# A 31-tap convolution on VectorE as three 16-tap filters over half the outputs each, in a hybrid encoder layer

## The chip, the core and the metric

One core of one Trainium2 chip runs the whole layer. The metric is the device time of one execution in microseconds (us). Two timed runs of the kernel before gave 1527.39 and 1528.0 us, median 1527.7. One more execution was profiled: it took 1526.56 us, and its instructions span 1524.8 us. All rows below come from that execution, with times counted from its first instruction.

## What is computed

The layer takes x (2048 tokens by 1024 channels, float32) and a conditioning vector c:

- h = RMSNorm(x) * (1 + scale(c)) + shift(c), then z = h @ W_in, cut into six parts of 1024 columns: a, a_glu, a_gate, u, v, b_gate.
- Group A: a * sigmoid(a_glu); then a depthwise convolution of 31 taps along the tokens (every channel has its own 31 weights, 15 tokens of zero padding on either side) plus a bias; then LayerNorm over the channels, silu, times silu(a_gate).
- Group B: u * (W_s LN(v) + b) over chunks of 128 tokens, times silu(b_gate).
- out = RMSNorm(x + gate(c) * (concat(A, B) @ W_out)).

For the change only the convolution matters, and the way the kernel forms its matrix products in the stage before it. With g the padded input of one channel and w its weights, the convolution is y[t] = bias + sum over i of w[i] * g[t + i], i = 0 to 30.

## The kernel before, in words

**Stages.** The tokens are handled in two halves of 1024 (hf = 0, 1). For each half the kernel forms h, then v (v_half), then runs 20 units: eight conv_in units (a and a_glu for channel block j of 128), eight gmlp units (u and b_gate) and four conv_gate units (a_gate). After both halves comes the output stage: the 16 token tiles of 128 are put into five groups of 3, 4, 4, 3 and 2 (GROUPS). The products of Group B's columns with W_out for groups 1 to 4 go first, and their partial sums are stored (part_out). Then for each group in turn Group A's rows are normalised (norm, a generator whose pieces are started by step() between tiles), split and multiplied (by_rows for group 0, by_tile for the others), and out_tile adds the residual, normalises and stores.

**A unit.** One unit makes two blocks of 128 output channels for 1024 tokens with seven products M1 to M7 (a Strassen-like scheme, L370 to L399), each of them 12 matmuls of 512 columns, because each operand is kept as a high and a low part (split, L129). It uses three PSUM banks p, t, q out of six. On TensorE the order is M1, then M4 of the unit before it (flush), M5, M6, M2, M3, M7. Before the change ScalarE copies M1 from p to SBUF (m1, L379), TensorE makes M6 in q, VectorE adds m1 to q in place (L384), ScalarE copies the sum out (u2, L385), and M7 later accumulates onto q.

**The convolution.** conv(hf, j) (L417) handles one channel block of one half. It loads g from DRAM (dG, written by conv_in), starts acc on ScalarE with the first tap and the bias (L429), adds the other 30 taps on VectorE, each one scalar_tensor_tensor over all n outputs (L431), and stores acc to DRAM (dC, L432). The first half's outputs end at token CUT = 1008, so that they need only the first half's input; the second half has 1040. There are two g buffers (pool gc) and one acc buffer (pool acc). The loads and the store of conv are issued by the POOL queue, one behind the other: the store of block j stands before the load of block j + 2.

**Order of work.** A scheduler orders each engine's instructions when the kernel is built, by priority and by its own simulated times; each engine then runs its list in that order. conv is under low() (tc.high_priority with an offset of -6000): its instructions come after any other work that is ready at that time, and so fill what VectorE has free. norm(2), the normalisation for tokens 896 to 1407, needs the convolution of all eight channel blocks of both halves, as do norm(3) and norm(4); norm(0) and norm(1) need the first half alone.

**Other users of the buffers touched.** Pool ct (five tiles of 128x512 before) holds m1, m5, u2 of the units, vm of gmlp, the raw weights of v_half (rv), Group B's rows on the way to the output stage (yb), and tm of out_tile.

Of the kernel before, what the change touches and what calls it, by code (L numbers as in the profile page):

```python
# [8 lines left out]
F32 = mybir.dt.float32  # L9
F32R = mybir.dt.float32r  # L10
AF = mybir.ActivationFunctionType
ALU = mybir.AluOpType
# [3 lines left out]
P = 128  # L16
D = 1024
KC = D // P
KH = KC // 2
S = 2048  # L20
T = 1024
NTT = T // P
W = 31
# [1 line left out]
EPS = 1e-6  # L25
NG = 512
LATE = 6000
CUT = T - PAD - 1
CSPAN = [(0, CUT), (CUT, S - CUT)]
GROUPS = [(0, 3), (3, 4), (7, 4), (11, 3), (14, 2)]  # L30

# [7 lines left out]
def hybrid_layer_kernel(  # L39
# [29 lines left out]
    gcp = pool("gc", 2)  # L69
    accp = pool("acc", 1)  # L70
    vcp = pool("vc", 1)
    ctp = pool("ct", 5)
    sqp = pool("sq", 1)
    tabs = pool("tabs", 2)
    small = pool("small", 4)
# [13 lines left out]
    def ct(name, dt=F32):  # L89
        return ctp.tile([P, NG], dt, tag="ct", name=name)  # L90
# [16 lines left out]
    c_sb = const.tile([P, KC], F32, name="c_sb")  # L107
    bss_sb = const.tile([P, KC, 2], F32, name="bss_sb")
    cw_sb = const.tile([P, KC, W], F32, name="cw_sb")
    ident = const.tile([P, P], F32, name="ident")  # L110
    ones = const.tile([P, P], F32, name="ones")
    csil = const.tile([P, KC], F32, name="csil")
# [170 lines left out]
    def v_half(hf, between=lambda: None):  # L283
        for r, pairs in enumerate(((("A11", "B1"), ("A12", "B2")), (("S1", "B1"), ("A22", "Bd")))):
            name = f"v{hf}{r}"
            ps = [[(bank if 2 * t + g < 6 else xbank)(f"pv_{hf}_{r}_{t}_{g}") for g in range(2)] for t in range(4)]
            for k in range(KH):
                for i, (b, typ) in enumerate(pairs):
                    for g in range(2):
                        s = v_op(typ, k, g, name)  # L290
                        st, sp = (k, i) == (0, 0), (k, i) == (KH - 1, 1)
                        for t in range(4):
                            a0, a1 = (H[b, k][:, q, t * P : (t + 1) * P] for q in range(2))
                            nc.tensor.matmul(ps[t][g], a0, s[:, 0, :], start=st, stop=False)
                            nc.tensor.matmul(ps[t][g], a0, s[:, 1, :], start=False, stop=False)
                            nc.tensor.matmul(ps[t][g], a1, s[:, 0, :], start=False, stop=sp)
            if r == 0:
                between()
            st = sm(f"vst_{name}", 16)
            sums, mean, var = st[:, 0:8], st[:, 8:12], st[:, 12:16]  # L300
            sq = sm(f"vsq_{name}", 8)
            vt = []
            for t in range(4):
                v = flat(slot(f"vt_{name}_{t}"))
                for g in range(2):
                    act(v[:, g * NG : (g + 1) * NG], ps[t][g], AF.Copy, accum_out=sums[:, 4 * g + t : 4 * g + t + 1])
                vt.append(v)
            TT(out=mean, in0=sums[:, 0:4], in1=sums[:, 4:8], op=ALU.add)
            TS(out=mean, in0=mean, scalar1=-1.0 / D, scalar2=None, op0=ALU.mult)
            for t in range(4):  # L310
                for g in range(2):
                    act(
                        ct(f"vq_{name}_{t}_{g}"),
                        vt[t][:, g * NG : (g + 1) * NG],
                        AF.Square,
                        bias=mean[:, t : t + 1],
                        accum_out=sq[:, 4 * g + t : 4 * g + t + 1],
                    )
            TT(out=var, in0=sq[:, 0:4], in1=sq[:, 4:8], op=ALU.add)
            TS(out=var, in0=var, scalar1=1.0 / D, scalar2=EPS, op0=ALU.mult, op1=ALU.add)  # L320
            rs = rstd_of(var, 4, name)
            nmr = sm(f"nmr_{name}", 4)
            TT(out=nmr, in0=mean, in1=rs, op=ALU.mult)
            for t in range(4):
                act(vt[t], vt[t], AF.Identity, bias=nmr[:, t : t + 1], scale=rs[:, t : t + 1])
                nc.sync.dma_start(dV[hf][4 * r + t].rearrange("p j d -> p (j d)"), vt[t])
# [30 lines left out]
    def product(ps, m, s, first):  # L357
        for k in range(KH):
            h = H[BLK[m], k]
            w0, w1 = (s[:, q, k * P : (k + 1) * P] for q in range(2))  # L360
            mm = lambda w, a, st, sp: nc.tensor.matmul(ps, w, a, start=st, stop=sp, skip_group_check=True)  # L361
            mm(w0, h[:, 0, :], first and k == 0, False)
            mm(w0, h[:, 1, :], False, False)
            mm(w1, h[:, 0, :], False, k == KH - 1)
# [7 lines left out]
    def unit(hf, key, cx, cy, start, finish):  # L372

        name = f"{hf}_{key[0]}{key[1]}"
        ws = weights(key, cx, cy, name)
        p, t, q = (bank(f"p{n}_{name}") for n in "ptq")
        m1, m5, u2 = (ct(f"{n}_{name}") for n in ("m1", "m5", "u2"))
        product(p, "M1", next(ws), True)
        act(m1, p, AF.Copy)  # L379
        flush()  # L380
        product(t, "M5", next(ws), True)
        act(m5, t, AF.Copy)
        product(q, "M6", next(ws), True)
        TT(out=q, in0=q, in1=m1, op=ALU.add)  # L384
        act(u2, q, AF.Copy)  # L385
        product(p, "M2", next(ws), False)
        y = start()
        product(t, "M3", next(ws), False)
        TT(out=y[:, :NG], in0=t, in1=u2, op=ALU.add)
        product(q, "M7", next(ws), False)  # L390
        TT(out=y[:, NG:], in0=q, in1=m5, op=ALU.add)
        last = next(ws)

        def rest():
            product(q, "M4", last, False)
            finish(p, q, y)

        pending.append(rest)
# [18 lines left out]
    def conv(hf, j):  # L417
        c0, n = CSPAN[hf]
        with low():
            g = gcp.tile([P, 1072], F32, tag="gc", name=f"gc_{hf}_{j}")  # L420
            if hf == 0:
                nc.gpsimd.memset(g[:, 0:PAD], 0.0)
                nc.gpsimd.dma_start(g[:, PAD : PAD + T - 1], dG[0][j][:, : T - 1])
            else:
                nc.gpsimd.memset(g[:, n + PAD : n + 2 * PAD], 0.0)
                nc.gpsimd.dma_start(g[:, : 2 * PAD + 1], dG[0][j][:, c0 - PAD :])
                nc.gpsimd.dma_start(g[:, 2 * PAD + 1 : n + PAD], dG[1][j])
            acc = accp.tile([P, 1040], F32, tag="acc", name=f"acc_{hf}_{j}")[:, :n]
            act(acc, g[:, 0:n], AF.Identity, bias=convb[:, j : j + 1], scale=cw_sb[:, j, 0:1])  # L429
            for i in range(1, W):  # L430
                STT(out=acc, in0=g[:, i : i + n], scalar=cw_sb[:, j, i : i + 1], in1=acc, op0=ALU.mult, op1=ALU.add)  # L431
            nc.gpsimd.dma_start(dC[hf][j], acc)  # L432

    def conv_gate(hf, i):
# [185 lines left out]
        for k in range(KH):  # L620
            H[b, k] = None
    c_row = vcp.tile([P, D], F32, tag="vc", name="c_row")
    rows0 = accp.tile([P, 1040], F32, tag="acc", name="rows0")[:, :D]
    nc.sync.dma_start(c_row[0:1, :], c[None, :])
    nc.gpsimd.memset(ones, 1.0)
    act(sm("warm", 1), ones[:, 0:1], AF.Silu)
# [13 lines left out]
    def x_home(hf):  # L640

        xs = []
        for k in range(KH):
            if k < 2:
                t = rawp.tile([P, 2, D], F32, tag="raw", name=f"x{hf}_{k}")
                xs.append((t[:, 0, :], t[:, 1, :]))
            elif k == 2:
                xs.append([hpool.tile([P, D], F32, tag=f"H_{b}_3", name=f"x{hf}_{b}") for b in ("S3", "S2")])
            elif hf == 0:
                xs.append([gcp.tile([P, 1072], F32, tag="gc", name=f"x0_{k}_{i}")[:, :D] for i in range(2)])  # L650
            else:
                xs.append([ek(f"x1_{k}_{i}") for i in range(2)])
        return xs
# [37 lines left out]
    for hf in range(2):  # L691
        if hf:
            for k in range(KH):
                h_scale(xs[k], rows1, k, B0)
                h_parts(xs[k], k, ("A1",))
            v_half(1, lambda: second_block(xs, rows1))
        for j in range(KC):
            conv_in(hf, j)
            if j:
                conv(hf, j - 1)  # L700
        flush()
        conv(hf, KC - 1)
        for j in range(KC):
            gmlp(hf, j)
            if hf == 0:
                x1_square(j)
            else:
                w_prepare(KC + j)
                w_prepare(j)
        if hf == 0:  # L710
            x1_rstd()
        for i in range(KC // 2):
            if hf == 0 and i == 1:
                rows1 = sqp.tile([P, D], F32, tag="sq", name="rows1")
                x1_rows(rows1)
            conv_gate(hf, i)
        flush()
        if hf == 0:
            xs = x_home(1)
            for k in range(KH):  # L720
                for sl in (B0, B1):
                    x_load(1, xs, k, sl)
# [154 lines left out]
```

## Time and profile before

| what | us |
|---|---|
| two timed runs, median | 1527.7 |
| the profiled execution | 1526.56 |
| its span, first to last instruction | 1524.8 |
| TensorE (PE) matmul busy in the span | 1376.1 |
| VectorE (DVE) busy | 1265.3 |
| ScalarE (ACT) busy | 546.7 |
| busy time of the convolution's taps (L431, VectorE), 480 instructions | 614.0 |

Busy times are unions of an engine's instructions. Matmuls overlap one another, so a busy TensorE is not one at its peak; what is to be read is where it is idle. "PEld" is TensorE's weight load, POOL is GpSimd, SP is SyncE.

### The profile page before, as it was taken

Reading aid. Unit: us, or ns where it says so; the run is one execution under the profiler, and the core shown is the slowest. Engines: PE = TensorE matmul, PEld = TensorE weight load, DVE = VectorE, ACT = ScalarE, POOL = GpSimd, SP = SyncE. Lnnn points to the kernel's source line nnn. Section 1 sums busy time; section 2 is a strip of 40 time slices with the busy share of each in tenths; the row PEclk is TensorE's granted clock in tenths of the full one; section 3 lists DMA queues with packets and bytes.
Section 4 is the critical chain, followed back from the end, with each engine's and each line's share of the span. In section 5 each row is a group of like instructions: output and inputs, shape, how many; then the busy total and the mean of one; then the engine's idle time right before and its main releaser. Section 6 shows DMA issues by size and latency. Waiting matters only on the chain. (4 is left out here: it accounts for less than half of the span.)

```text
span 1524.8 us, 17428 instructions
## 1 busy us (share of the span) xinstructions
PE 1376.1 (90%) x6036; PEld 1119.9 (73%) x6036; DVE 1265.3 (83%) x1741; ACT 546.7 (36%) x973; POOL 33.5 (2%) x82
## 2 busy tenths in 40 slices
PE   2988999999999999999999999998999999306796
PEld 1767888888888888778888888786888888304675
DVE  7952699999999989687888897969898889976765
ACT  4563643443334435432112222222424313204533
POOL 0000000000000000000000000000000000000000
PEclk9999999999999999999999999999999999757998
DMA  8976987789888794787769999999954762513422
GB/s 285 364 250 243 380 333 287 285 305 328 281 313 315 290 342 154 270 306 259 247 216 347 349 395 361 352 335 335 322 175 130 251 220 97 179 63 97 151 90 77
DMA packets 139849, 395.71 MB, mean 260 GB/s; under 512 B 14897, under 2 KB 49873, under 8 KB 135666
## 3 DMA queue, kind: packets, MB, share of 16 engines
q1 hardware_dynamic: 133618, 369.68, 67.2%
q0 software_dynamic: 6144, 24.93, 4.4%
q8 instruction: 47, 0.77, 0.2%
q14 instruction: 40, 0.33, 0.1%
HBM read 234.65 MB, written 159.91 MB: 259 GB/s over the span
## 5 line engine op out<-in xcount | busy, mean ns | idle before, releaser
L431 DVE SCALAR_TENSOR_TENSOR acc<-gc,cw_sb,acc 128x1008 f32<-128x1008 f32 (+1 forms) x480 | 614.0, 1279 | 25.6 <-ACT acc L429 20.6
L574 PE MATMUL po<-wr,y 128*128 128x512 f32 x512 | 205.0, 402 | 22.7 <-ACT y L130 22.7
L575 PE MATMUL po<-wr,y 128*128 128x512 f32 x512 | 203.6, 399 | 0.0
L576 PE MATMUL po<-wr,y 128*128 128x512 f32 x512 | 197.4, 394 | 0.0
L574 PEld LDWEIGHTS po<-wr,y 128*128 128x128 f32 x512 | 99.1, 194 | 47.6 <-ACT y L130 25.5
L575 PEld LDWEIGHTS po<-wr,y 128*128 128x128 f32 x512 | 99.0, 193 | 21.2 <-issue 0.5
L576 PEld LDWEIGHTS po<-wr,y 128*128 128x128 f32 x512 | 96.9, 189 | 20.8 <-issue 0.5
L361 PE MATMUL pp_a<-H_A,w_a_M 128*128 128x512 f32 x384 | 95.0, 393 | 1.2 <-ACT m_a L379 1.1
L361 PE MATMUL pq_a<-H_S,w_a_M 128*128 128x512 f32 x384 | 94.9, 392 | 1.2 <-ACT w_a_M L130 1.2
L361 PE MATMUL pt_u<-H_S,w_u_M 128*128 128x512 f32 x384 | 95.7, 396 | 0.0
L361 PE MATMUL pp_u<-H_A,w_u_M 128*128 128x512 f32 x384 | 95.4, 393 | 0.0
L361 PE MATMUL pq_u<-H_S,w_u_M 128*128 128x512 f32 x384 | 94.7, 394 | 0.0
L361 PE MATMUL pt_a<-H_S,w_a_M 128*128 128x512 f32 x384 | 93.6, 391 | 0.0
L361 PEld LDWEIGHTS pq_a<-H_S,w_a_M 128*128 128x128 f32 x384 | 71.9, 188 | 17.6 <-ACT w_a_M L130 1.6
L361 PEld LDWEIGHTS pp_a<-H_A,w_a_M 128*128 128x128 f32 x384 | 71.8, 188 | 17.5 <-ACT m_a L379 1.5
L361 PEld LDWEIGHTS pt_a<-H_S,w_a_M 128*128 128x128 f32 x384 | 72.1, 188 | 15.8
L361 PEld LDWEIGHTS pp_u<-H_A,w_u_M 128*128 128x128 f32 x384 | 72.0, 188 | 15.6
L361 PEld LDWEIGHTS pq_u<-H_S,w_u_M 128*128 128x128 f32 x384 | 71.9, 188 | 15.6
L361 PEld LDWEIGHTS pt_u<-H_S,w_u_M 128*128 128x128 f32 x384 | 71.0, 188 | 14.6
L130 ACT ACTIVATE w_u_M<-raw_u 128x512 fp32r<-128x512 f32 x56 | 34.0, 627 | 66.6 <-DVE raw_u L343 14.6
L509 PE MATMUL pmean<-sq,ones 128*128 128x384 f32 (+2 forms) x10 | 6.1, 698 | 57.3 <-DVE sq L506 57.3
L131 DVE TENSOR_TENSOR w_a_M<-raw_a,w_a_M 128x512 fp32r<-128x512 f32 x56 | 37.3, 685 | 23.8 <-ACT w_a_M L130 23.6
(221 smaller groups left out, 2307.1 us busy)
## 6 DMA issues: line engine op xcount, KB each, us to landing
wv_B<-dW_B SPq DMA_DIRECT2D x32, 512.0 KB, 6.4
dW_o<-ws SPq DMA_DIRECT2D x16, 1024.0 KB, 7.2
wr<-dW_o SPq DMA_DIRECT2D x16, 1024.0 KB, 7.8
wa<-in_wa_ss_dram SPq DMA_DIRECT2D x16, 512.0 KB, 5.3
dW_B<-wv_B SPq DMA_DIRECT2D x16, 512.0 KB, 5.4
raw_a<-in_w_main_dram SPq DMA_DIRECT2D x16, 512.0 KB, 7.2
dV<-vt_v SPq DMA_DIRECT2D x16, 512.0 KB, 7.7
dG<-g SPq DMA_DIRECT2D x16, 512.0 KB, 5.7
```

The costliest lines, as they stand in the source:

```text
L130: act(s[:, 0, :], src, AF.Copy)
L131: TT(out=s[:, 1, :], in0=src, in1=s[:, 0, :].bitcast(F32), op=ALU.subtract)
L361: mm = lambda w, a, st, sp: nc.tensor.matmul(ps, w, a, start=st, stop=sp, skip_group_check=True)
L431: STT(out=acc, in0=g[:, i : i + n], scalar=cw_sb[:, j, i : i + 1], in1=acc, op0=ALU.mult, op1=ALU.add)
L509: nc.tensor.matmul(pm[:, :n], ones, rows, start=True, stop=True)
L574: nc.tensor.matmul(ps, yh, hi, start=st, stop=False, skip_group_check=True)
L575: nc.tensor.matmul(ps, yh, lo, start=False, stop=False, skip_group_check=True)
L576: nc.tensor.matmul(ps, yl, hi, start=False, stop=sp, skip_group_check=True)
```

## The change

Outputs are taken in pairs of blocks of 16 tokens: within each 32 outputs the first 16 are the "even" half (h = 0) and the last 16 the "odd" half (h = 1). With H0 the taps 0 to 15 and H1 the taps 16 to 30, and with X0, X1, X2 the inputs at a pair's start, 16 and 32 further on, the two halves are H0 X0 + H1 X1 and H0 X1 + H1 X2. The changed conv works out M = (H0 + H1) X1 once into the even half of acc (one tap on ScalarE, 15 on VectorE), overwrites g with the difference g[t] - g[t + 16] (one VectorE subtraction), copies M to the odd half of acc (ScalarE), adds H0 of the difference to the even half (16 taps) and -H1 of the difference to the odd half (15 taps). Every tap now walks n / 2 outputs in runs of 16 with gaps of 16. The summed taps (cws) and the negated H1 are made once, by three small VectorE instructions. CUT becomes 992 so that both spans (992 and 1056) are multiples of 32.

In the units, ScalarE copies M1 from p straight into bank q (L379 of before, other target), M6 accumulates onto it, and VectorE's addition (L384) is gone. Pool ct has four tiles instead of five. What only widens a tile of pool gc or acc is left out of the diff here.

```diff
+HT = 16
-CUT = T - PAD - 1
+CUT = (T - PAD - 1) // (2 * HT) * 2 * HT
...
-    ctp = pool("ct", 5)
+    ctp = pool("ct", 4)
...
+    cws = const.tile([P, KC, HT], F32, name="cws")
...
-        m1, m5, u2 = (ct(f"{n}_{name}") for n in ("m1", "m5", "u2"))
+        m5, u2 = (ct(f"{n}_{name}") for n in ("m5", "u2"))
         product(p, "M1", next(ws), True)
-        act(m1, p, AF.Copy)
+        act(q, p, AF.Copy)
         flush()
         product(t, "M5", next(ws), True)
         act(m5, t, AF.Copy)
-        product(q, "M6", next(ws), True)
-        TT(out=q, in0=q, in1=m1, op=ALU.add)
+        product(q, "M6", next(ws), False)
         act(u2, q, AF.Copy)
...
             if hf == 0:
                 nc.gpsimd.memset(g[:, 0:PAD], 0.0)
-                nc.gpsimd.dma_start(g[:, PAD : PAD + T - 1], dG[0][j][:, : T - 1])
+                nc.gpsimd.dma_start(g[:, PAD : n + 2 * PAD], dG[0][j][:, : n + PAD])
             else:
                 nc.gpsimd.memset(g[:, n + PAD : n + 2 * PAD], 0.0)
-                nc.gpsimd.dma_start(g[:, : 2 * PAD + 1], dG[0][j][:, c0 - PAD :])
-                nc.gpsimd.dma_start(g[:, 2 * PAD + 1 : n + PAD], dG[1][j])
+                nc.gpsimd.dma_start(g[:, : n + PAD - T], dG[0][j][:, c0 - PAD :])
+                nc.gpsimd.dma_start(g[:, n + PAD - T : n + PAD], dG[1][j])
...
-            act(acc, g[:, 0:n], AF.Identity, bias=convb[:, j : j + 1], scale=cw_sb[:, j, 0:1])
-            for i in range(1, W):
-                STT(out=acc, in0=g[:, i : i + n], scalar=cw_sb[:, j, i : i + 1], in1=acc, op0=ALU.mult, op1=ALU.add)
+            pairs = lambda t, h: t.rearrange("p (m r) -> p m r", r=2 * HT)[:, :, h * HT : (h + 1) * HT]
+
+            def taps(h, at, tab, i0, n_taps):
+                for i in range(i0, n_taps):
+                    STT(
+                        out=pairs(acc, h),
+                        in0=pairs(g[:, i : i + n], at),
+                        scalar=tab[:, j, i : i + 1],
+                        in1=pairs(acc, h),
+                        op0=ALU.mult,
+                        op1=ALU.add,
+                    )
+
+            act(pairs(acc, 0), pairs(g[:, :n], 1), AF.Identity, bias=convb[:, j : j + 1], scale=cws[:, j, 0:1])
+            taps(0, 1, cws, 1, HT)
+            ne = n + HT - 2
+            TT(out=g[:, :ne], in0=g[:, :ne], in1=g[:, HT : HT + ne], op=ALU.subtract)
+            nc.scalar.copy(pairs(acc, 1), pairs(acc, 0))
+            taps(0, 0, cw_sb[:, :, :HT], 0, HT)
+            taps(1, 1, cw_sb[:, :, HT:], 0, W - HT)
             nc.gpsimd.dma_start(dC[hf][j], acc)
...
+        if hf == 0:
+            nc.vector.tensor_copy(out=cws, in_=cw_sb[:, :, :HT])
+            TT(out=cws[:, :, : W - HT], in0=cws[:, :, : W - HT], in1=cw_sb[:, :, HT:], op=ALU.add)
+            TS(out=cw_sb[:, :, HT:], in0=cw_sb[:, :, HT:], scalar1=-1.0, scalar2=None, op0=ALU.mult)
```

## Rows read from the trace of the kernel before

**Rows 1.** The page's parts 1 and 2: busy time; 40 slices of 38.1 us.

```profile
PE 1376.1 (90%) x6036; PEld 1119.9 (73%) x6036; DVE 1265.3 (83%) x1741; ACT 546.7 (36%) x973; POOL 33.5 (2%) x82
...
PE   2988999999999999999999999998999999306796
```

**Rows 2.** TensorE's timeline around its long idle stretch: start, us, what, idle before.

```profile
1310.14 0.39 PE L576 MATMUL po<-wr,y 128*128 128x512 f32 x1
1363.57 2.05 PE L509 MATMUL pmean<-sq,ones 128*128 128x512 f32 x2 [53.04 <-DVE sq L506]
...
1390.18 0.80 PE L574 MATMUL po<-wr,y 128*128 128x512 f32 x1 [8.26 <-ACT y L130]
```

**Rows 3.** Busy time by stretch: PE, PEld, DVE, ACT, POOL, clock, DMA share, GB/s.

```profile
1250.00:1310.00 60.00, 60.00 (x267) 49.69 (x266) 58.63 (x87) 19.71 (x43) 2.67 (x5) 1.00 0.33 114
1310.00:1356.00 46.00, 0.53 (x3) 0.11 (x1) 44.36 (x52) 3.68 (x11) 1.84 (x4) 0.56 0.32 111
```

**Rows 4.** The same of the convolution's tile acc alone: DVE, ACT, POOL.

```profile
1250.00:1310.00 60.00, 36.54 (x29) 1.26 (x1) 0.53 (x1) 1.00 0.33 114
1310.00:1356.00 46.00, 37.46 (x29) 0.00 (x0) 0.25 (x1) 0.56 0.32 111
```

**Rows 5.** The chain of waits: the last convolution block's store.

```profile
1355.75 2.92 DMA dC<-acc
```

**Rows 6.** Groups by line with their shapes: count, busy us, mean ns, idle before.

```profile
L431 DVE SCALAR_TENSOR_TENSOR acc<-gc,cw_sb,acc 128x1040 f32<-128x1040 f32 x240 | 311.1, 1296 | 10.5 <-ACT acc L429 7.6
L431 DVE SCALAR_TENSOR_TENSOR acc<-gc,cw_sb,acc 128x1008 f32<-128x1008 f32 x240 | 302.9, 1262 | 15.1 <-ACT acc L429 13.0
...
L467 DVE SCALAR_TENSOR_TENSOR vm<-px,cols_sb,bt 128x512 f32<-128x512 f32 x32 | 23.6, 744 | 0.9 <-PE px L465 0.7
...
L131 DVE TENSOR_TENSOR ws<-wo,ws 128x1024 fp32r<-128x1024 f32 x16 | 19.5, 1216 | 0.6 <-ACT ws L130 0.6
...
L384 DVE TENSOR_TENSOR pq_a<-pq_a,m_a 128x512 f32<-128x512 f32 x16 | 11.1, 694 | 6.9 <-PE pq_a L361 6.9
L384 DVE TENSOR_TENSOR pq_u<-pq_u,m_u 128x512 f32<-128x512 f32 x16 | 11.1, 693 | 6.8 <-PE pq_u L361 6.7
...
L384 DVE TENSOR_TENSOR pq_s<-pq_s,m_s 128x512 f32<-128x512 f32 x8 | 5.5, 693 | 10.8 <-PE pq_s L361 10.8
```

**Rows 7.** VectorE's timeline, second half's v stage: taps in a chain and between others.

```profile
611.50 1.27 DVE L431 SCALAR_TENSOR_TENSOR acc<-gc,cw_sb,acc 128x1008 f32<-128x1008 f32 x1
612.69 0.15 DVE L323 TENSOR_TENSOR nmr_v<-vst_v,r_v 128x4 f32<-128x4 f32 x1
612.80 9.09 DVE L431 SCALAR_TENSOR_TENSOR acc<-gc,cw_sb,acc 128x1008 f32<-128x1008 f32 x7
```

**Rows 8.** The tile acc: durations min/median/max, and an idle cause with its count.

```profile
L431 DVE SCALAR_TENSOR_TENSOR acc<-gc,cw_sb,acc x480: 1253/1276/1304, 198.5 to 1354.2; 128x1008 f32<-128x1008 f32 x80, 128x1040 f32<-128x1040 f32 x80
...
  ACT acc L429: 20.6, 8
```

**Rows 9.** Groups by line: ScalarE copies out of and into PSUM.

```profile
L772 ACT ACTIVATE po<-pi 128x512 f32<-128x512 f32 x26 | 15.6, 599 | 43.4 <-DVE tm L587 43.3
...
L379 ACT ACTIVATE m_a<-pp_a 128x512 f32<-128x512 f32 x16 | 9.5, 592 | 15.4 <-PE pp_a L361 15.3
```

**Rows 10.** TensorE's timeline, first unit of the second half: M6, then M2.

```profile
645.74 2.92 PE L361 MATMUL pq_a<-H_S,w_a_M 128*128 128x512 f32 x12
649.73 3.03 PE L361 MATMUL pp_a<-H_A,w_a_M 128*128 128x512 f32 x12 [1.08 <-ACT m_a L379]
```

**Rows 11.** ScalarE's timeline there: the copy of M1.

```profile
649.11 0.57 ACT L379 ACTIVATE m_a<-pp_a 128x512 f32<-128x512 f32 x1
```

**Rows 12.** VectorE's timeline: norm(3)'s first addition.

```profile
1388.61 0.55 DVE L504 TENSOR_TENSOR sq<-Y 128x384 f32<-128x384 f32 x1
```

**Rows 13.** TensorE's timeline where group 3 follows group 2.

```profile
1436.27 0.39 PE L576 MATMUL po<-wr,y 128*128 128x512 f32 x1
...
1446.32 0.80 PE L574 MATMUL po<-wr,y 128*128 128x512 f32 x1 [8.33 <-ACT y L130]
```

More of the change, by code (lines that the diff above doesn't have):

```diff
@@ L419, in conv @@
         with low():
-            g = gcp.tile([P, 1072], F32, tag="gc", name=f"gc_{hf}_{j}")
+            g = gcp.tile([P, 1088], F32, tag="gc", name=f"gc_{hf}_{j}")
             if hf == 0:
                 nc.gpsimd.memset(g[:, 0:PAD], 0.0)
-                nc.gpsimd.dma_start(g[:, PAD : PAD + T - 1], dG[0][j][:, : T - 1])
+                nc.gpsimd.dma_start(g[:, PAD : n + 2 * PAD], dG[0][j][:, : n + PAD])
             else:
                 nc.gpsimd.memset(g[:, n + PAD : n + 2 * PAD], 0.0)
-                nc.gpsimd.dma_start(g[:, : 2 * PAD + 1], dG[0][j][:, c0 - PAD :])
-                nc.gpsimd.dma_start(g[:, 2 * PAD + 1 : n + PAD], dG[1][j])
-            acc = accp.tile([P, 1040], F32, tag="acc", name=f"acc_{hf}_{j}")[:, :n]
-            act(acc, g[:, 0:n], AF.Identity, bias=convb[:, j : j + 1], scale=cw_sb[:, j, 0:1])
-            for i in range(1, W):
-                STT(out=acc, in0=g[:, i : i + n], scalar=cw_sb[:, j, i : i + 1], in1=acc, op0=ALU.mult, op1=ALU.add)
+                nc.gpsimd.dma_start(g[:, : n + PAD - T], dG[0][j][:, c0 - PAD :])
+                nc.gpsimd.dma_start(g[:, n + PAD - T : n + PAD], dG[1][j])
+            acc = accp.tile([P, 1056], F32, tag="acc", name=f"acc_{hf}_{j}")[:, :n]
+            pairs = lambda t, h: t.rearrange("p (m r) -> p m r", r=2 * HT)[:, :, h * HT : (h + 1) * HT]
[16 more added lines that the diff above has]
+            taps(1, 1, cw_sb[:, :, HT:], 0, W - HT)
             nc.gpsimd.dma_start(dC[hf][j], acc)
@@ L622, in hybrid_layer_kernel @@
     c_row = vcp.tile([P, D], F32, tag="vc", name="c_row")
-    rows0 = accp.tile([P, 1040], F32, tag="acc", name="rows0")[:, :D]
+    rows0 = accp.tile([P, 1056], F32, tag="acc", name="rows0")[:, :D]
     nc.sync.dma_start(c_row[0:1, :], c[None, :])
@@ L649, in x_home @@
             elif hf == 0:
-                xs.append([gcp.tile([P, 1072], F32, tag="gc", name=f"x0_{k}_{i}")[:, :D] for i in range(2)])
+                xs.append([gcp.tile([P, 1088], F32, tag="gc", name=f"x0_{k}_{i}")[:, :D] for i in range(2)])
             else:
```

## The prediction, made before the changed kernel was run

> **What bounds the kernel now.** I read the page's busy times and slices first. TensorE is at 9 tenths or more in nearly all slices up to the 34th, then come 3, 0 and 6 [rows 1]. So the kernel is bound by TensorE for some 1250 us, then something else stops TensorE, and then a tail follows that is neither full nor empty. The next view is TensorE's timeline at the hole: the last matmul of group 1 starts at 1310.14, the next full work, group 2's, at 1390.18. Between them stand norm(2)'s few matmuls, the first of which waited 53.04 us for VectorE's sums [rows 2]. The hole is 1390.2 - 1310.5 = 79.7 us.
>
> What fills it on VectorE? In 1310 to 1356 VectorE is busy 44.36 of 46 us while TensorE has 0.53 [rows 3], and 37.46 us of that are the convolution's taps [rows 4]. The chain of waits goes through the store of the last convolution block, issued at 1355.75 [rows 5]; 34.4 us later norm(2) has given TensorE its first operand. So the convolution, which runs only in VectorE's free time, ends too late: of the 614.0 us that it takes in its two shapes [rows 6], 37.5 are left when TensorE runs dry. The stretch before shows how slowly it is worked off while TensorE is busy: 36.54 us of taps in 1250 to 1310, with VectorE at 58.63 of 60 us [rows 3, 4].
>
> **What the change does to the convolution.** Per channel block, 30 taps over 1008 or 1040 outputs become 46 taps (15 + 16 + 15) over 496 or 528, and one subtraction over 1006 or 1070 elements. The nearest row for a half tap is vm, the same operation over 512 elements at 744 ns; with the two full lengths (1262 and 1296 ns) it lies on one line, 1.05 ns an element and some 210 ns fixed [rows 6]. That gives 727 ns for 496 and 761 ns for 528. Sixteen blocks: 8 x 46 x 0.727 + 8 x 46 x 0.761 = 547.6 us. The subtraction is priced by a 1024-element one at 1216 ns [rows 6]: 16 x 1.22 = 19.5 us. Together 567 us against 614.0: 47 us less, though the elements walked fall by a quarter; the fixed part is now paid 736 times, not 480.
>
> How sure is that? Two bounds from the rows. In a chain of taps one starts every (9.09 - 1.27) / 6 = 1.303 us, longer than its 1.27; where another instruction stands between, the next starts after 1.19 us [rows 7]. So the cost above the 1.05 us of pure walking is 0.25 us in a chain and 0.14 between others. A block walks 7 x 1024 elements less (7.5 us), pays 16 more fixed parts and one subtraction: at 0.25 that saves 16 x (7.5 - 4.0 - 1.2) = 37 us, at 0.14 it saves 65. I take 47. No row shows a VectorE operation that walks runs of 16 with gaps. From below, nothing makes it faster than its length; from above, nothing in this trace excludes that it costs as much as a walk over the whole span, 1279 ns. I take the price by length, since that row is of the same operation, and keep the other for a rival.
>
> Here the Trainium skill (Vector Engine (DVE) Microarchitecture Reference, section 5.2 Measured stream behaviour on trn2) has a rule that cuts both ways: runs of 16 adjacent words with a hop between them go at full rate, but pairs of words that start on an odd word go at 1.30 instead of 1.054 ns an element. Of the 46 taps 23 start at an odd offset; if they paid that over their whole length, the sum would be an estimated 23 x 16 x 512 x 0.246 ns = 46 us dearer and the convolution's saving gone. In the trace, 15 of the 30 taps of a block start odd, and yet all 480 durations lie between 1253 and 1304 ns, around the means of the two shapes [rows 8]; but those are single long runs.
>
> The ScalarE tap halves (it is off the path). The new ScalarE copy, M to the odd half, is about 0.6 us by ScalarE's copies of 512 [rows 9] and runs beside the 1.2 us subtraction, which needs the same taps and not the copy. The cover is gone where ScalarE's queue is late: the next tap on VectorE waits for the copy, and behind it everything on VectorE. At the start of a block, where the first tap waits for ScalarE today, VectorE lost 20.6 us in 8 cases, 2.6 each [rows 8]. So 0 to 16 x 2.6 = 41 us; I take 0, as that wait includes the store of the one acc buffer, and this one does not. Block starts keep their wait as it is. The three preparing instructions (about 128 columns each) are under 1 us. CUT = 992 leaves norm(0) and norm(1) on the first half alone, and the loads stay two or fewer per block on POOL's queue behind the same stores.
>
> **What it does to the units.** VectorE's 40 additions at L384 go: 11.1 + 11.1 + 5.5 = 27.7 us busy, and before them VectorE stood idle 6.9 + 6.8 + 10.8 = 24.5 us for TensorE's M6 [rows 6]. I count the busy time alone; the idle time comes back in part at the next addition, which waits for M3. The copy of M1 into q costs ScalarE what the copy to SBUF did: PSUM to SBUF is 592 ns, SBUF to PSUM 599 [rows 9]; from PSUM to PSUM no row shows, and I take 0.6.
>
> A wait is added: M6 needs this copy, where before only L384 needed it. Usually M4 of the unit before and M5 stand between, two products of some 2.9 us [rows 10]. In the first unit of a half there is no M4, and ScalarE is still busy with the v stage: in the second half the copy ran at 649.11 to 649.68, while M6 had started at 645.74 [rows 10, 11]. TensorE would stand 3.9 us in place of the 1.08 that M2 waited there, 2.9 more. The first half's first unit I put the same, 6 us in all; bounds 0 (another order) and 40 units x 0.6 = 24.
>
> Four ct tiles instead of five: a unit now takes two, gmlp two more, so the cover is as before. The v stage and the loads of yb lose a tile of prefetch; I take 0 and keep 5 us for the range.
>
> **The sum.** VectorE is freed of 47 + 27.7 - 1 = 74 us before the convolution's end. The last 37.5 us of taps, those after 1310, go first; the other 36.5 are what 1250 to 1310 holds [rows 4]. So the convolution would end near 1250. What is late next? norm(2) took 34.4 us with VectorE free; norm(3), worked off between tiles, took from 1388.61 [rows 12] to 1446.32 [rows 13], 58 us. 1250 + 58 = 1308: norm(2) is ready about when TensorE ends group 1, at 1310.5 + 6 = 1316.5. Then a seam remains like the one between groups 2 and 3, from 1436.7 to 1446.3, some 10 us [rows 13], and group 2 starts near 1327 instead of 1390. The tail behind it (1390.2 to 1524.8, 134.6 us) has no convolution in it and stays. Span 1327 + 134.6 = 1462, with the 1.8 us around it 1464; the profiled execution was 1.1 us under the median of the timed runs, so 1465.
>
> Once the convolution is early, more earliness is worth nothing: TensorE's own end sets the time. The forecast holds while the freed time is about 60 us or more; below that each freed microsecond is worth about one.
>
> **The rivals.**
>
> *The gain is cut to half.* Half taps that cost 0.80 us instead of 0.745 (0.055 x 736 = 40 us), or the copy waiting 2.6 us in every block (41 us), leave some 34 us freed. The convolution then ends 34 x 46 / 37.46 = 42 us sooner, at 1314, norm(2) is ready about 40 us later, at 1354, and 36 us are saved: 1490. For it: the missing row for gapped walks and the chain bound of 37. Against: 0.80 would be their spacing in a pure chain (0.54 + 0.25), and VectorE has other work to put between. The skill's odd-start price above would land near here.
>
> *Slower: a gapped walk is dear.* The place is the 736 half taps. Up to (614.0 + 27.7 - 20.5) / 736 = 0.844 us each VectorE is no worse off; from 0.844 + 30 / 736 = 0.885 the end comes over 2% later. At 1.279, a walk over the whole span, VectorE has 941 - 621 = 320 us more; of VectorE's idle time (1524.8 - 1265.3 = 260 us, much of it at the two ends [rows 1]) perhaps a quarter takes up some of it, and the time is near 1780. For it: no row. Against: 744 ns is also the price of vm, whose operands are views of four pieces, one repeated [rows 6].
>
> *No change: taps go by places.* The scheduler may put one tap into each gap of VectorE's list as before; then 46 taps need half as many places again, and VectorE idles more. The convolution ends near 1340 and the time is about 1515. Against: chains of seven taps stand in the list where nothing else is ready [rows 7].
>
> **How the numbers follow.** Forecast 0.67, half gain 0.17, no change 0.08, dear walks 0.06, better than 1440 (seams closing too) 0.02. A measurement of this kernel can tell about 2%, 30.6 us, from no change. Faster by over that: 0.67 + 0.02 + three quarters of the half gain, 0.81. Within: 0.12. Slower: 0.07. The forecast's own cases run from 1440 (no seam, no new stall) to 1480; the range goes on through the half gain to 1510, leaving out the dear walks, most of no change and little else.
>
> **What would show it.** Right: half taps at 0.72 to 0.77 us with 736 of them, no L384, the last dC store near 1250 to 1275, and TensorE's hole before group 2 down to 10 to 20 us. The new wait shows as TensorE idle before M6 for L379, a few us in the first units. Wrong: half taps over 0.8 us; a last store after 1310; VectorE's taps waiting for the copy in mid block; or a hole of the same length with the convolution done, which would mean that norm(2) itself is what comes late.

## The result, and the profile after

The changed kernel takes 1460.29 us (median of 2 runs, 1459.58 to 1461.0) against 1527.7: ratio 0.9559, 95% interval 0.9518 to 0.96. The prediction was 1465, in a range of 1440 to 1510, faster with 0.81. The profiled execution spans 1459.2 us. First the page's busy times and TensorE's 40 slices (36.5 us each):

```profile
PE 1363.8 (93%) x6036; PEld 1120.7 (77%) x6036; DVE 1174.6 (80%) x1976; ACT 545.6 (37%) x989; POOL 33.7 (2%) x82
...
PE   2879999999999999999999999999889999997786
```

The slices 3, 0, 6 of [rows 1] are gone. TensorE's timeline where group 2 follows group 1, to be held against [rows 2]:

```profile
1314.57 0.39 PE L595 MATMUL po<-wr,y 128*128 128x512 f32 x1
1314.79 1.02 PE L162 MATMUL pr_cn<-dg_cn,ones 128*128 128x512 f32 x2
1325.08 0.80 PE L593 MATMUL po<-wr,y 128*128 128x512 f32 x1 [9.27 <-ACT y L132]
```

Group 1 ends at 1315.0, group 2 starts at 1325.08. The hole of 79.7 us has become a seam of 10.1 us, like the one of [rows 13]. The new line numbers are L381 for the copy of M1, L435 for the taps, L444 and L448 for the ScalarE tap and the copy in a block, L593 to L595 for the output matmuls. The stretch of [rows 3] once more, all engines (PE, PEld, DVE, ACT, POOL, clock, DMA share, GB/s), then the convolution's tile acc alone (DVE, ACT, POOL) there and in the stretch before it, the view of [rows 4]:

```profile
1250.00:1310.00 60.00, 60.00 (x268) 49.48 (x267) 39.31 (x91) 23.61 (x55) 2.67 (x5) 1.00 0.43 137
```

```profile
1080.00:1250.00 170.00, 67.01 (x92) 2.09 (x3) 1.08 (x2) 1.00 0.60 210
1250.00:1310.00 60.00, 0.00 (x0) 0.00 (x0) 0.00 (x0) 1.00 0.43 137
```

No tap is left after 1250, and VectorE has room: 39.31 of 60 us where it was 58.63. The POOL timeline has the last block's store where [rows 5] had it at 1355.75:

```profile
1204.64 0.54 POOL L451 DMA_DIRECT2D dC<-acc  x1 [56.70 <-DVE acc L435]
```

The taps by shape, against [rows 6] (count, busy us, mean ns, idle before), and the tile acc's durations (ns min/median/max), against [rows 8]:

```profile
L435 DVE SCALAR_TENSOR_TENSOR acc<-gc,cw_sb,acc 128x528 f32<-128x528 f32 x248 | 175.1, 762 | 0.5
L435 DVE SCALAR_TENSOR_TENSOR acc<-gc,cw_sb,acc 128x496 f32<-128x496 f32 x248 | 170.8, 729 | 0.2
...
L435 DVE SCALAR_TENSOR_TENSOR acc<-gc,cws,acc 128x528 f32<-128x528 f32 x120 | 92.0, 767 | 14.7 <-ACT acc L444 12.1
L435 DVE SCALAR_TENSOR_TENSOR acc<-gc,cws,acc 128x496 f32<-128x496 f32 x120 | 87.7, 731 | 14.5 <-ACT acc L444 13.1
```

```profile
L435 DVE SCALAR_TENSOR_TENSOR acc<-gc,cw_sb,acc x496: 701/741/771, 220.8 to 1203.6; 128x496 f32<-128x496 f32 x83, 128x528 f32<-128x528 f32 x83
L435 DVE SCALAR_TENSOR_TENSOR acc<-gc,cws,acc x240: 724/746/772, 199.6 to 1165.9; 128x496 f32<-128x496 f32 x60, 128x528 f32<-128x528 f32 x60
...
L448 ACT COPY acc<-acc x16: 592/616/637, 219.4 to 1166.7; 128x496 f32<-128x496 f32 x8, 128x528 f32<-128x528 f32 x8
...
  ACT acc L444: 25.2, 7
```

Half taps cost 729 to 767 ns, the price by length (727 and 761). But look at the first number behind the bar, which is a union: the 496 taps of the second and third filter take 345.9 us, 0.697 each, less than one lasts, and the 240 of the first filter 179.7, 0.749 each. VectorE's timeline shows it in stretches without other work, as [rows 7] did:

```profile
738.65 5.58 DVE L435 SCALAR_TENSOR_TENSOR acc<-gc,cws,acc 128x528 f32<-128x528 f32 x7
...
757.69 9.59 DVE L435 SCALAR_TENSOR_TENSOR acc<-gc,cw_sb,acc 128x528 f32<-128x528 f32 x14
```

Seven taps of the first filter start (5.58 - 0.77) / 6 = 0.80 us apart, fourteen of the other two (9.59 - 0.76) / 13 = 0.68. The taps fell from 614.0 to 525.6 us; with 16 subtractions of some 1.24 us (19.8) the convolution is 545 us.

### The profile page after: what moved, and what is told of

The parts are those of the page before. It is cut to its first block, busy times and chain, and to the rows that moved or that the text cites. A ratio compares the mean times of both kernels' runs of the same rounds, so it can differ in the third digit from the quotient of the medians.

```text
span 1459.2 us, 17680 instructions
## 1 busy us (share of the span) xinstructions
PE 1363.8 (93%) x6036; PEld 1120.7 (77%) x6036; DVE 1174.6 (80%) x1976; ACT 545.6 (37%) x989; POOL 33.7 (2%) x82
## 4 chain that ended last, share of the span: by engine, by line
PE 87%; DVE 5%; DMA 3%; ACT 3%; issue 1%; SPq 0%; DVEq 0%; ACTq 0%
PE pq_u L363 9%; PE pq_a L363 9%; PE po L593 8%; PE po L594 8%; PE po L595 8%; PE pt_u L363 6%; PE pp_u L363 6%; PE pp_a L363 6%; PE pt_a L363 6%; PE pq_s L363 4%; PE pv L296 3%; PE pv L297 3%; PE pv L298 3%; PE pt_s L363 3%; PE pp_s L363 3%; PE px L484 2%
## 5 line engine op out<-in xcount | busy, mean ns | idle before, releaser
L435 DVE SCALAR_TENSOR_TENSOR acc<-gc,cw_sb,acc 128x496 f32<-128x496 f32 (+1 forms) x496 | 345.9, 745 | 0.7
L593 PE MATMUL po<-wr,y 128*128 128x512 f32 x512 | 206.3, 404 | 29.3 <-ACT y L132 23.7
L435 DVE SCALAR_TENSOR_TENSOR acc<-gc,cws,acc 128x496 f32<-128x496 f32 (+1 forms) x240 | 179.7, 749 | 29.1 <-ACT acc L444 25.2
L595 PE MATMUL po<-wr,y 128*128 128x512 f32 x512 | 197.3, 393 | 0.0
L593 PEld LDWEIGHTS po<-wr,y 128*128 128x128 f32 x512 | 99.5, 194 | 54.1 <-ACT y L132 25.8
L595 PEld LDWEIGHTS po<-wr,y 128*128 128x128 f32 x512 | 97.1, 190 | 21.0 <-issue 0.5
```

The source lines that it names most:

```text
L435: STT(out=pairs(acc, h), in0=pairs(g[:, i : i + n], at), scalar=tab[:, j, i : i + 1], in1=pairs(acc, h), op0=ALU.mult, op1=ALU.add,)
L593: nc.tensor.matmul(ps, yh, hi, start=st, stop=False, skip_group_check=True)
L595: nc.tensor.matmul(ps, yl, hi, start=False, stop=sp, skip_group_check=True)
```

## The experiments

**The convolution alone (e1) and the units alone (e2).** e1 is the changed kernel with the old units; e2 the kernel before with the new units, both with four ct tiles.

```diff
 e1, from the changed kernel
-        act(q, p, AF.Copy)
+        act(m1, p, AF.Copy)
...
-        product(q, "M6", next(ws), False)
+        product(q, "M6", next(ws), True)
+        TT(out=q, in0=q, in1=m1, op=ALU.add)
```

> The new convolution with the old units (M1 copied to SBUF, VectorE's addition kept), four ct tiles. Theory 'late convolution' (the time is set by whichever ends later, TensorE's own work or the convolution plus norm(2); a microsecond of VectorE freed before that is worth about one until the hole in front of group 2 is closed): the convolution alone frees 614 - 526 - 20 = 68 us, enough to close the hole, so 1458 to 1470 us, with the last dC store near 1255. Rival 'the units did it' (the gain comes from the shorter chain M6 to u2 and from TensorE's matmuls in the units, one every 227 ns after and 229 before): most of the gain is missing, 1500 or more.

> The old convolution of 30 full taps with the new units (M1 put into bank q by ScalarE), four ct tiles. Late convolution: 28 us of busy time freed on VectorE and up to 24 us of its waits, so the convolution ends 34 to 50 us sooner and the hole shrinks by as much: 1480 to 1495 us, with a hole of 30 to 45 us left. Rival 'the units did it': 1465 or less. Rival 'only the convolution counts': 1520 or more.

e1: 1456.99 us, ratio 0.952 (0.9501 to 0.9538). The convolution alone brings all of the gain. TensorE's timeline of e1 at the end of group 1:

```profile
1310.22 1.02 PE L162 MATMUL pr_cn<-dg_cn,ones 128*128 128x512 f32 x2
1320.51 0.79 PE L594 MATMUL po<-wr,y 128*128 128x512 f32 x1 [9.27 <-ACT y L132]
```

Its last store lay at 1222.7, 32 us earlier than the 1255 that the theory gave:

```profile
1222.70 0.54 POOL L452 DMA_DIRECT2D dC<-acc  x1 [63.55 <-DVE acc L436]
```

VectorE was idle for less of the time: up to 1200 us it was busy 1025.6 us in e1, where it had been busy 1010.2 in the kernel before and 1013.7 in the changed one. Which entries of its list filled the 15 us is open.

e2: 1506.5 us, ratio 0.985 (0.9835 to 0.9865), between the theory's window and the rival's; TensorE's timeline of e2 there:

```profile
1330.79 0.39 PE L575 MATMUL po<-wr,y 128*128 128x512 f32 x1
1341.92 2.04 PE L508 MATMUL pmean<-sq,ones 128*128 128x512 f32 x2 [10.74 <-DVE sq L505]
...
1369.52 0.79 PE L573 MATMUL po<-wr,y 128*128 128x512 f32 x1 [8.26 <-ACT y L130]
```

The last store moved from 1355.75 to 1330.68, by 25 us, and the hole shrank to 1369.5 - 1331.2 = 38 us. The time fell less than the hole, because TensorE came to the end of group 1 20 us later than before (1331.2 for 1310.5). Of these 20 us, 8 were lost up to the end of the units (1054.1 for 1046.5) and 13 behind it, in part by waits of 5.5, 2.3 and 2.2 us in the output stage; why this build's lists cost it that much is open.

**The kernel before with four ct tiles (e3).**

```diff
-    ctp = pool("ct", 5)
+    ctp = pool("ct", 4)
```

> The kernel before with four ct tiles instead of five and nothing else. Late convolution: the tile of prefetch costs the v stage or the loads of yb a few us of TensorE's time at most, and those are hidden behind the hole: 1524 to 1533 us. Rival 'a tile less is dear': 1535 or more. If the spacing of matmuls in the units (229 ns before, 227 after) comes from where the tiles lie in SBUF, it changes here too, at an unchanged time; if it comes from VectorE's additions in PSUM, it stays at 229.

1525.63 us, ratio 0.9977 (0.9968 to 0.9986). The tile costs nothing at the end of the run, because the hole hides it: TensorE ended group 1 at 1316.9 instead of 1310.5. The changed kernel has no such hole, and with five tiles it was not run. The matmul spacing stayed at 229 and 233 ns.

**Half taps in one run (e4).**

```diff
-pairs = lambda t, h: t.rearrange("p (m r) -> p m r", r=2 * HT)[:, :, h * HT : (h + 1) * HT]
+pairs = lambda t, h: t[:, h * (n // 2) : (h + 1) * (n // 2)]
```

> The changed kernel with half taps that walk the first or last half of the span in one run instead of runs of 16 with gaps (the convolution is another one then; counts and lengths are the same). 'Price by length': half taps stay at 729 and 762 ns within 5 ns, the time within 5 us. Rival 'gaps or odd starts cost something': they fall by 10 ns or more.

The output is another convolution then; counts and lengths are the same. 1461.21 us in one run. The taps by shape in e4:

```profile
L435 DVE SCALAR_TENSOR_TENSOR acc<-gc,cw_sb,acc 128x528 f32<-128x528 f32 x248 | 174.7, 758 | 0.5
L435 DVE SCALAR_TENSOR_TENSOR acc<-gc,cw_sb,acc 128x496 f32<-128x496 f32 x248 | 170.5, 726 | 0.2
L435 DVE SCALAR_TENSOR_TENSOR acc<-gc,cws,acc 128x528 f32<-128x528 f32 x120 | 91.9, 766 | 18.4 <-ACT acc L444 15.8
L435 DVE SCALAR_TENSOR_TENSOR acc<-gc,cws,acc 128x496 f32<-128x496 f32 x120 | 87.6, 730 | 14.3 <-ACT acc L444 13.0
```

726 to 730 and 758 to 766 ns, against 729 to 731 and 762 to 767 with gaps: 1 to 4 ns. Runs of 16 with gaps, odd starts among them, cost nothing that matters, and all 736 half taps of the changed kernel, of either length and start, lie between 701 and 772 ns. The Trainium skill's price for odd starts (Vector Engine (DVE) Microarchitecture Reference, section 5.2 Measured stream behaviour on trn2) is measured there on runs of two words; on runs of 16 this trace does not show it.

**More taps of weight 0 (e5: two per block, e6: five).**

```diff
             taps(1, 1, cw_sb[:, :, HT:], 0, W - HT)
+            for i in range(5):
+                STT(out=acc, in0=g[:, i : i + n], scalar=0.0, in1=acc, op0=ALU.mult, op1=ALU.add)
```

> The changed kernel with two more full-length taps of weight 0 at the end of every channel block: 32 taps of some 1.28 us, 41 us more work on VectorE; the output is the same. 'Late convolution': the last store moves from 1205 to some 1265 to 1285, norm(2) still comes about when TensorE ends group 1, so the time stays within 8 us of 1460. Rival 'VectorE's work always counts': 1460 + 41 = 1500.

> The same with five such taps a block: 80 taps, 102 us, a little more than the change freed (69 by the convolution, 28 by the additions). 'Late convolution': the last store lies near 1355 to 1365 again, the hole before group 2 is back, and the time is 1515 to 1540. Rival 'the gain came from elsewhere (the units, TensorE's matmul spacing)': 1500 or less.

e5: 39 us more taps (20.1 + 19.0), last store at 1243.8 (21 us before the window expected), time 1462.73 us, ratio 0.9569 (0.955 to 0.9589): free. e6: 97.7 us more (50.1 + 47.6), last store at 1347.6 (7 us before its window), 1520.81 us, ratio 0.9957 (0.9941 to 0.9973): all but 8 us of the gain is gone. The last stores of e5 and of e6:

```profile
1243.81 0.54 POOL L453 DMA_DIRECT2D dC<-acc  x1 [68.94 <-DVE acc L452]
```

```profile
1347.63 0.53 POOL L453 DMA_DIRECT2D dC<-acc  x1 [23.59 <-DVE acc L452]
```

TensorE's timeline of e6 has the hole of [rows 2] again:

```profile
1303.17 0.39 PE L597 MATMUL po<-wr,y 128*128 128x512 f32 x1
1355.56 2.05 PE L530 MATMUL pmean<-sq,ones 128*128 128x512 f32 x2 [52.00 <-DVE sq L527]
...
1382.17 0.80 PE L595 MATMUL po<-wr,y 128*128 128x512 f32 x1 [8.26 <-ACT y L132]
```

This is the case's main test: with the units, the ct tiles and the spacing of matmuls as in the changed kernel, giving VectorE back what was taken from it gives the time back, and not before the convolution's end comes too late for norm(2).

**One chain (e7).** The third filter is added to the even half, so the odd half keeps M.

```diff
-            taps(1, 1, cw_sb[:, :, HT:], 0, W - HT)
+            taps(0, 1, cw_sb[:, :, HT:], 0, W - HT)
```

> The changed kernel with the third filter added to the even half too, so that all 46 taps of a block are one chain of dependent taps (the odd half then keeps M alone; the convolution is another one). 'Two chains overlap': taps of the second and third filter start 0.65 to 0.68 us apart in the changed kernel because even and odd halves alternate; in one chain they start some 0.77 to 0.80 apart like the first filter's, L435's union rises from 526 to 560 to 580 us, the time stays within 8 us of 1460. Rival 'order and dependence do not matter': the union stays below 535.

1467.65 us in one run, last store at 1267.8. The taps of the second and third filter in e7:

```profile
L435 DVE SCALAR_TENSOR_TENSOR acc<-gc,cw_sb,acc 128x528 f32<-128x528 f32 x248 | 189.8, 765 | 5.6
L435 DVE SCALAR_TENSOR_TENSOR acc<-gc,cw_sb,acc 128x496 f32<-128x496 f32 x248 | 181.2, 731 | 3.9
```

Their union rose from 345.9 to 371.0 us, that of all taps from 526 to 551, less than the 560 to 580 expected, since many taps stand between other work in any case. Where taps follow taps, the direction is shown: twelve taps of the second and third filter start (9.61 - 0.77) / 11 = 0.80 us apart in e7, as the first filter's do, and 0.68 in the changed kernel. Independent halves overlap, one chain does not.

```profile
776.69 9.61 DVE L435 SCALAR_TENSOR_TENSOR acc<-gc,cw_sb,acc 128x528 f32<-128x528 f32 x12
```

**norm one tile earlier (e8), and with the old units (e11).** The seams that are left have ScalarE's y in front of them. In program order the last piece of norm(gi + 1) stands behind the last tile of group gi; these kernels pull it forward.

```diff
         for t in range(nt):
+            for _ in range(2 if t == 0 else 1):
+                step()
             ps = part_in(t0 + t)
             by_tile(ps, ys, 0, t, False, True)
             out_tile(t0 + t, ps)
-            step()
```

> The changed kernel with norm(gi + 1) worked off one tile earlier: two of its pieces before the first tile of group gi, one before each later tile, none after. Now that the convolution ends at 1205, VectorE has room for it. 'The seams are norm's last piece, which stands behind the last tile': the three seams of 9 to 10 us in front of groups 2, 3 and 4 fall to 3 us or less, 1435 to 1445 us. Rival 'the seams are the work itself (VectorE or the y tiles)': they stay, 1455 to 1465, or the pieces stop TensorE elsewhere.

> The new convolution with the old units, and norm(gi + 1) one tile earlier as in the run with the early norm. If the units' part is worth nothing once the convolution is off the end, this is 1432 to 1442 us, as the early norm with the new units (1438). If VectorE's 28 us of additions now stand in the way of the earlier norm, 1445 or more.

e8: 1438.04 us, ratio 0.9407 (0.9384 to 0.9431). TensorE's waits (us, times, longest) for that y, first in the changed kernel, then in e8:

```profile
PE po L593 <- ACT y L132: 23.7, 3, 9.3
```

```profile
PE po L593 <- ACT y L132: 7.8, 2, 6.5
```

Two of the three seams are gone; the one in front of group 4 is still 6.5 us, where 3 or less was expected.

e11: 1430.06 us, ratio 0.9356 (0.9341 to 0.9371), the fastest version here. So with the convolution off the end the units' part is worth nothing or less: e11 beats e8 by 8 us; e1 lay 3 us under the changed kernel, but their intervals overlap. Part of the 8 us is the start of the output stage (TensorE idle 7.1 us there in e11, 12.3 in e8); which entry of the lists makes it was not tried.

**The place of the H pieces (e9, e10).** The traces so far had shown something unlooked for: matmuls of the v stage and of the units follow one another faster after the change. One row here is a product of 12 matmuls; consecutive starts give its length. Before, then changed:

```profile
746.61 2.91 PE L361 MATMUL pp_a<-H_A,w_a_M 128*128 128x512 f32 x12
749.35 2.91 PE L361 MATMUL pt_a<-H_S,w_a_M 128*128 128x512 f32 x12
```

```profile
740.49 2.88 PE L363 MATMUL pq_a<-H_S,w_a_M 128*128 128x512 f32 x12
743.21 2.88 PE L363 MATMUL pp_a<-H_A,w_a_M 128*128 128x512 f32 x12
```

2.74 and 2.72 us. In the v stage it is 233.5 and 227 ns a matmul. Two kernels put 64 bytes in front of the H pieces, the SBUF tiles of h and of its sums that these matmuls read (the pools of the output stage, which take their place later, move along):

```diff
     dram = pool("dram", 1, space=DRAM)
+    pad = pool("pad", 1)
+    nc.gpsimd.memset(pad.tile([P, 16], F32, name="pad64"), 0.0)
```

> The changed kernel with one unused tile of 64 bytes a partition in front of the pool that holds the H pieces, so that all H pieces lie 64 bytes further on; nothing else. In the kernel before, in the one with four ct tiles and in the one with new units alone a matmul of the v stage follows the last after 233.5 ns and one of the units after 229; wherever the new convolution's tiles are in (they move H by 64 bytes modulo 128) it is 227 in both. 'Place of H': with the pad it is 233 and 229 again, TensorE ends some 12 us later (768 x 6.4 ns + 3360 x 2.2 ns), and the time is 1468 to 1475. Rival 'it is the convolution's taps on VectorE that slow TensorE': 227 stays, 1457 to 1464.

> The changed kernel itself once more, on the chip of the padded run and of the early norm with old units, to compare with: 1457 to 1464 us.

> The kernel before with the same 64 bytes in front of H. 'Place of H': matmuls every 227 ns in the v stage and the units, TensorE ends group 1 some 12 us earlier, near 1298; the time stays within 8 us of 1527, since the convolution sets the end there. Rival: 233 and 229 stay.

e9: 1471.83 us, ratio 0.9623 (0.9597 to 0.9648); the changed kernel on the same chip (e12): 1462.56, ratio 0.9567 (0.9551 to 0.9583). The pad costs 9 us and brings 233 ns back in the v stage and 230 in the units; the products shown take 2.80 us in e9:

```profile
743.16 2.96 PE L365 MATMUL pt_a<-H_S,w_a_M 128*128 128x512 f32 x12
745.96 2.96 PE L365 MATMUL pq_a<-H_S,w_a_M 128*128 128x512 f32 x12
```

e10 went the wrong way on both counts: 1542.2 us in one run, products of 2.80 us in place of 2.72,

```profile
739.02 2.96 PE L363 MATMUL pt_a<-H_S,w_a_M 128*128 128x512 f32 x12
741.82 1.80 PE L363 MATMUL pp_a<-H_A,w_a_M 128*128 128x512 f32 x7
```

and the time rose by 13 us though the convolution sets the end there. Its POOL timeline shows the last store 15.4 us later than in the kernel before.

```profile
1371.13 0.53 POOL L434 DMA_DIRECT2D dC<-acc  x1 [19.41 <-DVE acc L433]
```

So 'modulo 128' was wrong; and a slower TensorE does delay the convolution. VectorE's list is fixed, and its taps stand behind additions that wait for TensorE: by operations and tile names (buffer numbers left out), VectorE, ScalarE and TensorE have the same order of instructions in e10 as in the kernel before (and in e9 as in the changed kernel), so that only the pace differs.

## Why the prediction was right, point by point

*What bounds the kernel.* Right. e6 shows it by itself: 98 us of VectorE work restore the hole, 39 us cost nothing (e5). "Worth about one" below 60 us freed fits e2, where 28 us freed moved the last store by 25 us and the time by 22.5. What the prediction left out is that the hole was not a cover for TensorE: e10 lost on TensorE and paid in full. In the kernel before, TensorE's pace moves the convolution's end as well.

*The convolution's price.* Half taps came out at 729 to 767 ns for 727 and 761, and gaps are free (e4). The step that failed is "I take 47": 69 us were saved, 545 us in place of 567. The even and odd halves are independent after the first filter, and VectorE starts the next independent tap 0.68 us after the last, not 0.80. The upper bound of 65, worked out from taps between other work [rows 7], was the nearer one.

*The copy in the block.* The block's copy (L448) takes 616 ns and no wait for it shows in the tile's causes; taps waited 25.2 us in 7 cases for L444 at block starts, as they did before (20.6 in 8).

*The units.* L384 is gone, but the 27.7 us were not needed: e1 without them is as fast. The wait of M6 for the copy was priced at 6 us. ScalarE's L381 in the trace, and who waited for it:

```profile
L381 ACT ACTIVATE pq_a<-pp_a x16: 574/582/582, 152.4 to 773.3; 128x512 f32<-128x512 f32 x16
...
  PEld pq_a L363: 0.4, 1
```

0.4 us, once. The scheduler had moved the copy in front of the v stage's last squares, so that M6 of the second half's first unit starts with M5's end. That the order of the old list would stay was the wrong step.

*The sum.* Convolution's end: 1250 predicted, 1204.6 measured. With the true freed time, 69 + 28 us, the same way of counting (37.5 after 1310, 36.5 in 1250 to 1310, the rest at the rate of the stretch before) gives 1204. The stretch before, in the kernel before (tile acc, as in [rows 4]):

```profile
1080.00:1250.00 170.00, 81.62 (x63) 3.76 (x3) 1.07 (x2) 1.00 0.65 219
```

That this count meets 1204.6 so closely is luck in part: for e1, with 69 us freed, it gives 1258, and 1222.7 was measured; for e2, with 28, it gives 1322, and 1330.7 was measured. It takes VectorE's other work and its idle time as given, and the order of the lists moves both.

The earliness was worth nothing more, as the prediction said: TensorE's own end took over. That end was put at 1316.5 and came at 1315.0, but by errors that cancel. Where the units end and the output stage starts, before, then changed:

```profile
1043.43 3.04 PE L361 MATMUL pq_s<-H_A,w_s_M 128*128 128x512 f32 x12 [1.05 <-DVE sag L391]
1050.71 1.62 PE L509 MATMUL pmean<-sq,ones 128*128 128x384 f32 x2 [4.24 <-DVE sq L506]
```

```profile
1036.67 3.02 PE L363 MATMUL pq_s<-H_A,w_s_M 128*128 128x512 f32 x12 [1.01 <-DVE sag L392]
...
1045.94 0.76 PE L593 MATMUL po<-wr,y 128*128 128x512 f32 x1 [5.61 <-DMA wr<-dW_o]
...
1071.85 1.65 PE L162 MATMUL pr_cn<-dg_cn,ones 128*128 128x384 f32 x2 [5.88 <-DVE dg_cn L155]
```

TensorE was through with the units 6.8 us sooner (1039.7 for 1046.5): the 6 us of M6 waits did not come, and the H pieces' place, worth some 9 us by e9, had been priced by nobody. From there to the end of group 1 it took 275.3 us where it had taken 264.0. Of these 11.3 us more, 7.3 are idle time (11.5 for 4.2), and an estimated 3.4 went to its granted clock behind the second wait (0.88 of full in 1060 to 1072 and 0.75 in 1072 to 1080, 1.00 in both before; that is some 7 us at 1.2 GHz, the lower of its two levels). The four ct tiles, put at nothing, may have a share in this, as e3 hints; so does the order of the lists, since with the same units and ct tiles group 1 ended at 1303.6 in e6 and at 1321.0 in e7. Which of the two made it is open, and differences of a few us between versions are not shown to be VectorE's.

Seam 10.1 for 10, tail 1459.2 - 1325.1 = 134.1 for 134.6. At the old spacing of matmuls the change would have given about 1470 (the ratio of e9, 0.9623, on 1527.7), still inside the range.

*The rivals.* Dear walks are out by the taps' durations and e4. Taps by places is out: fourteen half taps stand in one row where VectorE is free. The half gain did not come, since neither the price nor the copy's wait rose.

## What to carry to other kernels

Work that fills an engine's free time cost nothing here until its end met the first stage that needs it (39 us more were free, 97.7 were not); price a change to it there, as freed time against the hole, and stop counting once another engine sets the end. In a chain of short VectorE instructions look for two independent chains: here a half tap started every 0.68 us instead of every 0.80. When one bound goes, look at the next one at once: the seams of 10 us in front of each group were cheap to close (e8, e11) once the convolution had left VectorE free; an earlier norm with the old convolution was not run.

## What the runs showed of the hardware

The spacing of the v stage's and the units' matmuls (128x512, float32) depends on where the H pieces lie in SBUF: in e9 and e10 nothing else differs but one memset and the place of the later pools. The table has the means of start-to-start times within one bank, worked out from the matmul starts of each trace; the shift of the H pieces is worked out from the tile sizes in each diff.

| kernel | H moved by, bytes | v stage, ns | units, ns |
|---|---|---|---|
| before | 0 | 233.5 | 229.3 |
| e3, e2 | -2048 | 233.4 | 229.5 |
| e9 | -1280 | 233.3 | 230 |
| changed, e1, e4 to e8, e11, e12 | -1344 | 227 | 227 |
| e10 | +64 | 233 | 233 |

The first three differ by multiples of 256 bytes and agree; 64 beyond such a multiple is slower in the units, 192 beyond is fast. Which operand of H, which bytes and why is open; other shifts were not tried. It is worth 9 us here (e9 against e12). The output stage's matmuls, which do not read H, start 227 ns apart in every one of these kernels.

A VectorE instruction starts later behind one whose output it needs: at 528 outputs taps start 0.80 us apart in a chain and 0.68 where two chains alternate (changed kernel, and e7 for one chain alone).
